# Two meta rows of an output projection, formed on VectorE and turned to channels through DRAM

## The chip, the cores and the metric

The kernel runs on one core of a Trainium2 chip. Its time is device time in microseconds. The kernel before was run three times: 1255.90, 1255.19 and 1255.82 us, a median of 1255.82. One more execution was taken with the hardware profiler, and all traces here are of such single executions.

A core has five engines that run their own instruction streams in order: TensorE (PE in the profile, with its weight loads as PEld), VectorE (DVE), ScalarE (ACT), GpSimd (POOL) and SyncE (SP), which issues most of the transfers. They wait for each other by semaphores.

## The reference

The program is one layer of a decoder trunk on 1,024 tokens of width 1,024, ahead of which stand 16 meta tokens. A first normalisation is followed by one wide projection; its columns feed an attention branch and a convolution branch, whose outputs are gated and added. What matters here comes after that:

```
mixed = sigmoid(g_attn) * y_attn + sigmoid(g_conv) * y_conv
h = layer_norm(ALPHA * h + mixed @ w_out, ln1_g, ln1_b)
up = causal_dwconv(h @ ffn_w_up, ffn_dw, ffn_dw_b)      # 3 taps: token t needs t-2, t-1, t
...
return h[:, N_META:]                                    # the meta tokens are dropped
```

The meta tokens' outputs are dropped, but the feed-forward convolution of the first real token reaches two tokens back. So after attention only the last two of the 16 meta tokens are still needed, and of those only `h` after `layer_norm`, as columns (one number per channel) at the left edge of the first token block. These are the two meta rows.

## The kernel before, in words

All matrix products are of float32 accuracy, made of reduced-precision passes: an operand is split into a rounded part `hi` and a remainder `lo` (`split`: a copy on ScalarE, then a subtraction on VectorE or GpSimd), and three products `hi*hi`, `hi*lo`, `lo*hi` are added in PSUM (`product`, L292 to L302).

The branches' projections run over eight stages `m` of 128 output channels (the loop that begins at L1080). In each, four column groups `g` of 256 or 258 tokens take two half-groups of 12 matmuls, one for each branch. Branch 0 writes to a pool of three PSUM banks, branch 1 to a pool of two. VectorE multiplies each with its gate (L1099, L1100), adds the two (L1101), and with ScalarE splits the sum into `mixed` (L1108, L1109). Group 0 holds the two meta tokens too; their 128 channels of `mixed` are kept in `pair[:, m]`, as `hi` and `lo`. During the same stages the eight 128x1024 tiles of `w_out` are loaded: four to parts of `FA` (`early`), two more that are split in stages 2 and 3 with the subtraction on GpSimd, and the last two into the weight buffers `wr`, split at the end.

Then come the row blocks (`out_rows`, L1230), in the order 3, -1, 7, 2, 6, 0, 4, 1, 5 (L1386). A row block is 128 tokens by 1,024 columns of `mixed @ w_out`, computed as two halves of 24 matmuls. VectorE adds the residual (L1253), takes statistics (L1254), and after a reciprocal root on ScalarE (L246) and three small steps it scales the rows (L1277). They are stored to `h1d` and, behind the first half of the next block, transposed on TensorE (`turn`, L1287) and copied by ScalarE into the feed-forward's operand in `FA` with gain and bias applied (L1300).

Block -1 is the two meta rows. Its stationary operand is `pair[:, k]`, four columns (two tokens, `hi` and `lo`) with `w_out`'s `hi`, and two columns with its `lo`: 16 matmuls of 512 columns in each half (L1264, L1265). ScalarE copies four rows out of PSUM (L1266); the lower two are moved beside the upper two by a small transfer, and VectorE adds both and the residual (L1270, L1272). After scaling, the two rows wait in a list and are turned together with block 2: eight transposes (L1287) and eight ScalarE steps of 128x2 into `edge`, which `edges` copies into the first two columns of `FA` (L1378).

After the row blocks follow the feed-forward's up products (L1499) and down products (L1637).

A scheduler orders each engine's instructions by their ranks and by its own estimate of when operands are ready; `after` adds an order between two instructions, `rank` sets a priority. The order is fixed when the kernel is built.

Of the kernel before, what the change touches and what calls it, by code (L numbers as in the profile page):

```python
# [99 lines left out]
def tile_hybrid_layer(  # L100
# [51 lines left out]
    sgd = dpool.tile([2, KC, P, U], F, name="sgd")  # L152
    h0d = dpool.tile([U, D], F, name="h0d")
    h1d = dpool.tile([S, D], F, name="h1d")
    fd = dpool.tile([FC, P, S], F, name="fd")

    td, sd = (dpool.tile([FH, P, 4 * 512], F, name=n) for n in ("td", "sd"))
# [860 lines left out]
    for g in range(3):  # L1018
# [8 lines left out]
    RW = wo_stack.enter_context(tc.tile_pool(name="rw", bufs=1, side="right", reuse_waits="tile")).tile(  # L1027
        [P, 2048], R, name="RW")
    RT = OB[:, 0:2048]


# [19 lines left out]
    def prep_wo(k, raw=None, behind=None):  # L1051
        if k < 4:
            hi, lo = OA[:, k * 2048:k * 2048 + 1024], OA[:, k * 2048 + 1024:k * 2048 + 2048]
        elif k < 6:
            hi, lo = ((RX, RW)[k - 4][:, x:x + 1024] for x in (0, 1024))
        else:
            hi, lo = (wsp_p.tile([P, D], R, name=n, tag=n) for n in ("whi", "wlo"))
        if raw is None:
            raw = wraw([P, D])
            load(raw, w_out_v[k])  # L1060
        split(raw, hi, lo, k < 4, behind)
        wo[k] = (hi, lo)

    pair = const.tile([P, KC, 4], R, name="pair")
    const.tile([P, 16], F, name="pad_e")
    g_next = [0]

    GS = [(FA, i * 516) for i in range(4)]
# [11 lines left out]
    for m in range(KC):  # L1080
        hi, lo = weights([P, KC, P], lambda raw: load(raw, w_ab[m]))

        def branch(i, g, tag, bufs):
            a, b = PG[g]
            ps = pat.tile([P, 512], F, name="ps_p", tag=tag, bufs=bufs)
            rhs = (oo, conv)[i]
            product(ps[:, :b - a], [(hi[:, 4 * i + k], lo[:, 4 * i + k], rhs(k, 0, a, b), rhs(k, 1, a, b))
                                    for k in range(4)])
            return ps[:, :b - a]

        def merge(g, psa, psb):
            a, b = PG[g]
            n = b - a
            with rank(RK_EVAC):
                t = gslot()[:, :, :n]
                ins = load(t, dram(sgd, m * P * U + a, [[U, P], [KC * P * U, 2], [1, n]]))

                ta, tb = t[:, 0], t[:, 1]
                nc.vector.scalar_tensor_tensor(ta, ta, 1.0, psa, OP.add, OP.mult)  # L1099
                nc.vector.scalar_tensor_tensor(tb, tb, 1.0, psb, OP.add, OP.mult)  # L1100
                nc.vector.tensor_tensor(ta, ta, tb, OP.add)  # L1101
                if g == 0:
                    nc.scalar.mul(pair[:, m, 0:2], ta[:, 0:2], 0.5)
                    nc.vector.scalar_tensor_tensor(pair[:, m, 2:4], ta[:, 0:2], 0.5, f32(pair[:, m, 0:2]),
                                                   OP.mult, OP.subtract)
# [3 lines left out]
                nc.vector.scalar_tensor_tensor(mixed2(g, m, 1), v, 0.5, f32(h), OP.mult, OP.subtract)  # L1109
            return ins, last_act  # L1110

        if m < KC - 1:
            for g in range(4):
                last_gate, last_act = merge(g, branch(0, g, "mm", 3), branch(1, g, "t", 2))
        else:
            pa = [branch(0, g, "mm", 3) if g < 3 else branch(0, g, "s", 2) for g in range(4)]
            for g in range(4):
                last_gate, last_act = merge(g, pa[g], branch(1, g, "t", 2))
        if m in (2, 3):
            raw = (FA[:, 4112:5136], OB[:, 3072:4096])[m - 2]  # L1120
            load(raw, w_out_v[m + 2])
            prep_wo(m + 2, raw, last_act)
        if m < 4:
            early.append(FA[:, W_AT[m]:W_AT[m] + 1024])
            after(load(early[m], w_out_v[m]), last_gate)
    for k in range(4):
        prep_wo(k, early[k])
    prep_wo(6)
    prep_wo(7)

# [99 lines left out]
    def out_rows(i, between=(), work=()):  # L1230


        n, u = (P, 2 + i * P) if i >= 0 else (2, 0)
        if n == P:
            o = r_next[0] % 2 * 1024
            r_next[0] += 1
            whole = RT[:, o:o + 1024]
            load(whole, h0d[u:u + n, :])
        else:
            whole = OB[:, 3072:4096]  # L1240
        r = whole[:n]
        order = WO_ORDER if i != 5 else (0, 1, 2, 3, 6, 7, 4, 5)
        turned = None
        st = small.tile([P, 2, 6], F, name="st")
        pin = line if i in (0, 4, 1, 5) else lambda ins: ins
        for half in range(2):
            hs = slice(half * 512, half * 512 + 512)
            ps = pat.tile([P, 512], F, name="ps_w", tag="mm", bufs=3)
            if n == P:
                last = product(ps, [(mixed(i, k, 0), mixed(i, k, 1), wo[k][0][:, hs], wo[k][1][:, hs])  # L1250
                                    for k in order], turned)
                with rank(RK_TURN):
                    pin(nc.vector.tensor_tensor(r[:, hs], ps, r[:, hs], OP.add))  # L1253
                    pin(nc.vector.bn_stats(st[:, half], r[:, hs]))  # L1254
                turned = None
                if len(between) > half:
                    turned = turn(*between[half], behind=[last])
                if half == 0:
                    for f, *x in work:
                        f(*x)  # L1260
                continue

            for j, k in enumerate(order):
                nc.tensor.matmul(ps[:4], pair[:, k], wo[k][0][:, hs], start=j == 0, stop=False)  # L1264
                last = nc.tensor.matmul(ps[:2], pair[:, k, 0:2], wo[k][1][:, hs], start=False, stop=j == KC - 1)  # L1265
            nc.scalar.copy(whole[:4, hs], ps[:4])  # L1266
        if n < P:
            q = FA[:4, 0:1024]
            load(q[0:2], h0d[0:2, :])
            nc.vector.tensor_tensor(r, r, q[0:2], OP.add)  # L1270
            load(q[0:2], whole[2:4])
            nc.vector.tensor_tensor(r, r, q[0:2], OP.add)  # L1272
        with rank(RK_TURN):
            (mu, rs), = ln_stats([(r, n)], half_stats=st if n == P else None)
            for a in (512, 0) if i == 5 else (None,):
                x = r if a is None else r[:, a:a + 512]
                ins = pin(nc.vector.tensor_scalar(x, x, mu, rs, OP.subtract, OP.mult))  # L1277
        if n == P:
            load(h1d[u - 2:u - 2 + P, :], r)
        return whole, n, ins  # L1280

    def turn(i, r, n, ins, banks=None, behind=None, upper=False):
        with rank(RK_TURN):
            for j, k0 in enumerate((4, 0) if upper else (0, 4)):
                ps = banks[j] if banks else pat.tile([P, 512], F, name="ps_h", tag="s", bufs=2)
                for k in range(4):
                    ins = nc.tensor.transpose(ps[:, k * P:(k + 1) * P], r[:, (k0 + k) * P:(k0 + k + 1) * P], ident)  # L1287
                    if behind:
                        after(ins, behind[-1])
                        behind.append(ins)  # L1290
                for k in range(k0, k0 + 4):
                    src = ps[:, (k - k0) * P:(k - k0) * P + n]
                    if n < P:
                        dst = edge[:, k]
                    else:
                        h, jj = divmod(i, 4)
                        sub = 0 if jj < 2 else 1
                        a = 2 + jj * P - SUB[sub][0]
                        dst = h1F(sub, h, k)[:, a:a + P]
                    nc.scalar.activation(dst, src, AF.Identity, bias=b1col(k), scale=g1col(k))  # L1300
        return behind[-1] if behind else None

# [71 lines left out]
    def edges():  # L1374
        with rank(RK_TURN):
            first, second = (FA[:, h * 2064:h * 2064 + 2064].rearrange("p (k n) -> p k n", n=258)[:, :, 0:2]
                             for h in range(2))
            nc.vector.tensor_copy(first, edge)  # L1378
            nc.vector.memset(second, 0.0)

    ahead = []
# [1 line left out]
            4: [(w_first, 2), (split_of, 1, BT2), (form_t4, 1)],  # L1383
            1: [(form_t3, 1), (w_first, 3)],
            5: [(form_t3, 0, EARLY), (form_t4, 0, EARLY)]}
    for i in (3, -1, 7, 2, 6, 0, 4, 1, 5):  # L1386
        if i == -1:
            two = (i, *out_rows(i))
# [402 lines left out]
```

## Time and profile before

| | |
|---|---|
| median of three runs | 1255.82 us |
| the profiled execution | 1255.65 us, its span 1253.9 us |
| mean granted TensorE clock | 0.999 |
| TensorE busy | 1241.6 us, 8,546 matmuls |
| VectorE busy | 1081.1 us, 1,876 instructions |
| ScalarE busy | 586.7 us, 1,056 instructions |
| GpSimd busy | 12.3 us, 11 instructions |
| projections / row blocks / up / down products | 416 to 510 / 503 to 610 / 607 to 1036 / from 1036 us |

How to read the lines: the page gives busy time, share of the span and count for each engine, and the span in 40 slices (tenths busy, 9 for 90% or more). A timeline row is start, duration, engine, line of the kernel, operation, output `<-` inputs, shape and count; brackets at its end give the idle time before it and what ended it. A matmul's duration runs from its start to the end of its way through the array; matmuls overlap, and the distance of two starts is what one costs. A group row gives count, busy us and the mean ns of one, then the idle time before. A wait row is engine and line `<-` what it waited for: total us, times, longest. A stretch row gives for each engine the busy us and count, then clock, share of the DMA engines and GB/s. A transfer row gives size and the median us from issue to landing.

### The profile page before, as it was taken

Reading aid. Unit: us, or ns where it says so; the run is one execution under the profiler, and the core shown is the slowest. Engines: PE = TensorE matmul, PEld = TensorE weight load, DVE = VectorE, ACT = ScalarE, POOL = GpSimd, SP = SyncE. Lnnn points to the kernel's source line nnn. Section 1 sums busy time; section 2 is a strip of 40 time slices with the busy share of each in tenths; the row PEclk is TensorE's granted clock in tenths of the full one; section 3 lists DMA queues with packets and bytes.
Section 4 is the critical chain, followed back from the end, with each engine's and each line's share of the span. In section 5 each row is a group of like instructions: output and inputs, shape, how many; then the busy total and the mean of one; then the engine's idle time right before and its main releaser. Section 6 shows DMA issues by size and latency. Waiting matters only on the chain.

```text
span 1253.9 us, 21702 instructions
## 1 busy us (share of the span) xinstructions
PE 1241.6 (99%) x8546; PEld 1174.7 (94%) x8546; DVE 1081.1 (86%) x1876; ACT 586.7 (47%) x1056; POOL 12.3 (1%) x11
## 2 busy tenths in 40 slices
PE   9999999999999999999999999999999999999997
PEld 8999999999999999788899999999999998888886
DVE  7899989999978786648899999999999986996697
ACT  7522345645465233235565555554455553545330
POOL 0000000000000010000000000000000000000000
PEclk9999999999999999999999999999999999999999
DMA  7293733332255565222145565553464569988722
GB/s 280 71 312 103 183 107 95 109 93 87 68 147 142 182 173 139 77 75 101 68 135 187 192 210 189 186 215 120 167 218 167 204 207 318 387 317 315 251 85 84
DMA packets 96152, 212.10 MB, mean 169 GB/s; under 512 B 10787, under 2 KB 35939, under 8 KB 95922
## 3 DMA queue, kind: packets, MB, share of 16 engines
q1 hardware_dynamic: 84282, 199.64, 48.1%
q10 hardware_dynamic: 11768, 11.08, 2.7%
q8 instruction: 67, 1.10, 0.4%
q14 instruction: 35, 0.29, 0.1%
HBM read 150.29 MB, written 62.70 MB: 170 GB/s over the span
## 4 chain that ended last, share of the span: by engine, by line
PE 95%; DVE 3%; DMA 1%; issue 1%; ACT 0%; SPq 0%; DVEq 0%
PE px L1499 15%; PE py L1499 10%; PE ps_x L1637 9%; PE ps_z L1637 7%; PE ps_z L300 7%; PE ps_z L301 7%; PE ps_z L296 7%; PE pw L1499 5%; PE pz L1499 5%; PE ps_p L301 2%; PE ps_p L296 2%; PE ps_p L300 2%; PE ps_w L301 2%; PE ps_w L296 2%; PE ps_w L300 2%; PE ps_z L512 2%
## 5 line engine op out<-in xcount | busy, mean ns | idle before, releaser
L665 DVE SCALAR_TENSOR_TENSOR FA<-cin,cols,FA 128x1026 f32<-128x1026 f32 x120 | 152.5, 1280 | 0.3
L296 PE MATMUL ps_z<-RHO,whi 128*128 128x384 f32 (+2 forms) x324 | 104.2, 322 | 0.0
L300 PE MATMUL ps_z<-RHC,whi 128*128 128x384 f32 (+2 forms) x324 | 104.1, 321 | 0.0
L300 PE MATMUL ps_z<-RHO,whi 128*128 128x384 f32 (+2 forms) x324 | 104.0, 321 | 0.0
L301 PE MATMUL ps_z<-RHC,wlo 128*128 128x384 f32 (+2 forms) x324 | 103.8, 320 | 0.0
L296 PE MATMUL ps_z<-RHC,whi 128*128 128x384 f32 (+2 forms) x324 | 103.7, 320 | 0.0
L301 PE MATMUL ps_z<-RHO,wlo 128*128 128x384 f32 (+2 forms) x324 | 103.7, 320 | 0.0
L267 ACT CAST whi<-wr 128x1024 fp32r<-128x1024 f32 x37 | 39.0, 1053 | 69.1 <-PE ps_z L300 52.2
L1317 ACT CAST RHO<-wr 128x512 fp32r<-128x512 f32 x94 | 56.9, 621 | 24.2 <-DVE wr L1335 13.6
L1318 DVE TENSOR_TENSOR RHO<-wr,RHO 128x512 fp32r<-128x512 f32 x94 | 63.8, 690 | 4.5 <-ACT RHO L1317 4.2
L296 PEld LDWEIGHTS ps_z<-RHO,whi 128*128 128x128 f32 x324 | 61.0, 188 | 0.6 <-issue 0.3
L296 PEld LDWEIGHTS ps_z<-RHC,whi 128*128 128x128 f32 x324 | 61.1, 188 | 0.2
L301 PEld LDWEIGHTS ps_z<-RHO,wlo 128*128 128x128 f32 x324 | 61.0, 188 | 0.2
L301 PEld LDWEIGHTS ps_z<-RHC,wlo 128*128 128x128 f32 x324 | 60.9, 188 | 0.2
L1335 DVE TENSOR_TENSOR wr<-wr 128x512 f32<-128x512 f32 x88 | 61.0, 693 | 0.2
L300 PEld LDWEIGHTS ps_z<-RHO,whi 128*128 128x128 f32 x324 | 61.0, 188 | 0.1
L300 PEld LDWEIGHTS ps_z<-RHC,whi 128*128 128x128 f32 x324 | 60.9, 188 | 0.1
L672 ACT ACTIVATE FA<-ps_z,cols 128x384 f32<-128x384 f32 (+1 forms) x48 | 26.1, 543 | 50.3 <-PE ps_z L301 49.3
L1511 ACT COPY FA<-px 128x514 f32<-128x514 f32 (+2 forms) x23 | 13.2, 572 | 73.3 <-PE px L1499 73.3
L270 DVE TENSOR_TENSOR wlo<-wr,whi 128x1024 fp32r<-128x1024 f32 x35 | 42.6, 1218 | 4.8 <-ACT whi L267 4.1
L1318 DVE TENSOR_TENSOR ws<-wr,ws 128x512 fp32r<-128x512 f32 x60 | 40.9, 690 | 5.5 <-ACT ws L1317 5.3
L1424 ACT ACTIVATE FA<-OB,cols 128x512 f32<-128x512 f32 x44 | 36.0, 817 | 13.6 <-DVE OB L1507 13.6
(466 smaller groups left out, 3520.7 us busy)
## 6 DMA issues: line engine op xcount, KB each, us to landing
wr<-in_w_up_dram SPq DMA_DIRECT2D x44, 512.0 KB, 3.8
wr<-in_w_z_dram SPq DMA_DIRECT2D x30, 512.0 KB, 4.3
fd<-FA SPq DMA_DIRECT2D x44, 256.0 KB, 2.0
OB<-in_w_down_dram SPq DMA_DIRECT2D x19, 512.0 KB, 4.8
qt<-qd SPq DMA_DIRECT2D x28, 256.0 KB, 4.1
sgd<-FA ACTq DMA_DIRECT2D x32, 192.0 KB, 3.1
td<-OB SPq DMA_DIRECT2D x12, 512.0 KB
sums<-fd SPq DMA_DIRECT2D x12, 512.0 KB
```

What stands on the lines that cost most here:

```text
L267: ins = nc.scalar.copy(hi, raw)
L270: return (nc.vector if quick else nc.gpsimd).tensor_tensor(lo, raw, f32(hi), OP.subtract)
L296: ins = nc.tensor.matmul(ps, ah, bh, start=i == 0, stop=False)
L300: nc.tensor.matmul(ps, ah, bl, start=False, stop=False)
L301: last = nc.tensor.matmul(ps, al, bh, start=False, stop=i == n - 1)
L665: nc.vector.scalar_tensor_tensor(acc[c], cin[:, j:j + U], wc, acc[c], OP.mult, OP.add)
L1317: nc.scalar.copy(hi, src)
L1318: ins = nc.vector.tensor_tensor(lo, src, f32(hi), OP.subtract)
L1335: ins = nc.vector.tensor_tensor(*x)
L1424: nc.scalar.activation(t, cc[:, 2:HW], AF.Identity, bias=ffw(3, o), scale=ffw(2, o))
L1499: ins = nc.tensor.matmul(o, x[:, ks], bmat(sub, q, hl, k), start=first and k + j == 0, stop=k == 3 and j == 2, skip_group_check=not first)
L1637: nc.tensor.matmul(banks[i], l[:, ts], r[:, ws], start=first and a and x + k == 0, stop=z and x == len(ops) - 1 and k == 2, skip_group_che ...
```

## The change

In words:

- `pair` is now float32 and holds the two tokens' channels as they are; the splitting step for it (L1104 before) goes.
- `two_rows(k)` forms the products on VectorE: for each of the two tokens, a tile `two` of 128x1024 takes up `w_out`'s raw tile `k` times the token's 128 channels, one factor per partition. Tile 0 is done on ScalarE, the others are multiply-adds on VectorE. Tiles 0 to 5 fall in the projection stages, tile 6 at their end, tile 7 behind block 3's scaling.
- The sum over partitions that is still missing is made by TensorE: both `two` tiles are split behind block 7's scaling, and eight matmuls with a selecting operand `sel` (ones in one column) bring token 0's sum to row 0 and token 1's to row 1.
- Block -1 moves behind block 2. Its rows come out of PSUM as two rows; one residual add is left of the two adds, and the small transfer goes.
- `turn` no longer treats two rows. The scaled rows are written to a DRAM buffer `ed` and read back in two transfers of 128x8 single elements into `edge`; `edges` applies gain and bias on VectorE.

```diff
-    pair = const.tile([P, KC, 4], R, name="pair")
+    pair = const.tile([P, KC, 4], F, name="pair")
+    sel = const.tile([P, 16], R, name="sel")
...
+    def two_rows(k, behind=None):
+        for t, a in enumerate(two_sum):
+            m = pair[:, k, t:t + 1]
+            if k == 0:
+                nc.scalar.activation(a, wo_raw[k], AF.Copy, scale=m)
+                continue
+            ins = nc.vector.scalar_tensor_tensor(a, wo_raw[k], m, a, OP.mult, OP.add)
+            if behind is not None:
+                after(ins, behind)
...
+        if m > 1:
+            with rank(RK_PROJ + 3000):
+                two_rows(m - 2)
...
-            for j, k in enumerate(order):
-                nc.tensor.matmul(ps[:4], pair[:, k], wo[k][0][:, hs], start=j == 0, stop=False)
-                last = nc.tensor.matmul(ps[:2], pair[:, k, 0:2], wo[k][1][:, hs], start=False, stop=j == KC - 1)
-            nc.scalar.copy(whole[:4, hs], ps[:4])
+            for j in range(4):
+                nc.tensor.matmul(ps[:2], sel[:, j // 2 * 2:j // 2 * 2 + 2], two_parts[j // 2][j % 2][:, hs],
+                                 start=j == 0, stop=j == 3)
+            nc.scalar.copy(r[:, hs], ps[:2])
...
+            load(ed, r)
+            for t in range(2):
+                load(edge[:, :, t], dram(ed, t * D, [[1, P], [P, KC]]))
...
-            nc.vector.tensor_copy(first, edge)
+            for t, c, op in ((edge, 58, OP.mult), (first, 66, OP.add)):
+                nc.vector.tensor_tensor(first, t, colA[:, c:c + KC].unsqueeze(2).to_broadcast([P, KC, 2]), op)
...
-    for i in (3, -1, 7, 2, 6, 0, 4, 1, 5):
+    for i in (3, 7, 2, -1, 6, 0, 4, 1, 5):
...
+        if i == 3:
+            two_rows(7, rows[2])
         if i == 7:
-            ahead.append(two)
+            for a, (hi, lo) in zip(two_sum, two_parts):
+                after(split(a, hi, lo, True), rows[2])
```

In the changed order of instructions, `edges` stands on VectorE between the two halves of block 6, and the eight `sel` matmuls stand between block 2's second half and block 6's first.

More of the change, by code (lines that the diff above doesn't have):

```diff
@@ L154, in tile_hybrid_layer @@
     h1d = dpool.tile([S, D], F, name="h1d")
+    ed = dpool.tile([2, D], F, name="ed")
     fd = dpool.tile([FC, P, S], F, name="fd")
@@ L1060, in prep_wo @@
             load(raw, w_out_v[k])
+        wo_raw[k] = raw
         split(raw, hi, lo, k < 4, behind)
         wo[k] = (hi, lo)
-    pair = const.tile([P, KC, 4], R, name="pair")
-    const.tile([P, 16], F, name="pad_e")
+    pair = const.tile([P, KC, 4], F, name="pair")
+    sel = const.tile([P, 16], R, name="sel")
+    nc.vector.memset(f32(sel), 0.0)
+    for t in range(2):
+        nc.vector.memset(f32(sel[:, 3 * t:3 * t + 1]), 1.0)
+    two_sum = [wo_p.tile([P, D], F, name=f"two{t}") for t in range(2)]
+    two_parts = [[OC[:, (2 * t + hl) * D:(2 * t + hl + 1) * D] for hl in range(2)] for t in range(2)]
+    wo_raw = {}
+    def two_rows(k, behind=None):
[7 more added lines that the diff above has]
+                after(ins, behind)
     g_next = [0]
@@ L1261, in out_rows @@
                 continue
-            for j, k in enumerate(order):
-                nc.tensor.matmul(ps[:4], pair[:, k], wo[k][0][:, hs], start=j == 0, stop=False)
-                last = nc.tensor.matmul(ps[:2], pair[:, k, 0:2], wo[k][1][:, hs], start=False, stop=j == KC - 1)
-            nc.scalar.copy(whole[:4, hs], ps[:4])
+            for j in range(4):
+                nc.tensor.matmul(ps[:2], sel[:, j // 2 * 2:j // 2 * 2 + 2], two_parts[j // 2][j % 2][:, hs],
+                                 start=j == 0, stop=j == 3)
+            nc.scalar.copy(r[:, hs], ps[:2])
         if n < P:
[L1268 to L1272, printed above, removed]
+            q = FA[:2, 0:1024]
+            load(q, h0d[0:2, :])
+            nc.vector.tensor_tensor(r, r, q, OP.add)
         with rank(RK_TURN):
@@ L1279, in out_rows @@
             load(h1d[u - 2:u - 2 + P, :], r)
+        else:
+            load(ed, r)
+            for t in range(2):
+                load(edge[:, :, t], dram(ed, t * D, [[1, P], [P, KC]]))
         return whole, n, ins
@@ L1291, in turn @@
                 for k in range(k0, k0 + 4):
[L1292 to L1299, printed above, removed]
+                    src = ps[:, (k - k0) * P:(k - k0 + 1) * P]
+                    h, jj = divmod(i, 4)
+                    sub = 0 if jj < 2 else 1
+                    a = 2 + jj * P - SUB[sub][0]
+                    dst = h1F(sub, h, k)[:, a:a + P]
                     nc.scalar.activation(dst, src, AF.Identity, bias=b1col(k), scale=g1col(k))
@@ L1385, in tile_hybrid_layer @@
             5: [(form_t3, 0, EARLY), (form_t4, 0, EARLY)]}
[L1386 removed]
+    for i in (3, 7, 2, -1, 6, 0, 4, 1, 5):
         if i == -1:
[L1388 removed]
+            out_rows(i)
             continue
```

8 lines of the change are left out of this document (4 added, 4 removed).

## The prediction

> **What bounds the kernel now.** I read the page's busy shares and slices first, then the chain that ended last, then TensorE's waits in the stage that the change touches.
>
> ```profile
> PE 1241.6 (99%) x8546; PEld 1174.7 (94%) x8546; DVE 1081.1 (86%) x1876; ACT 586.7 (47%) x1056; POOL 12.3 (1%) x11
> PE   9999999999999999999999999999999999999997
> PEclk9999999999999999999999999999999999999999
> PE 95%; DVE 3%; DMA 1%; issue 1%; ACT 0%; SPq 0%; DVEq 0%
> PE pw L1499 <- ACT FA L1300: 1.0, 1, 1.0
> ```
> TensorE is busy for 99% of the span and carries 95% of the last chain at full clock. The last line is the only wait of over 0.1 us that it has between 410 and 620 us, where the projections and the eight row blocks of `w_out` run. So a matmul taken out there is worth its whole slot, and a wait put in costs its whole length.
>
> **What TensorE loses and gains.** The timeline of TensorE around the meta rows:
>
> ```profile
> 515.48 0.40 PE L1264 MATMUL ps_w<-RX,pair 128*4 128x512 f32 x1
> ...
> 518.96 0.40 PE L301 MATMUL ps_w<-whi,RHC 128*128 128x512 f32 x1
> ...
> 524.06 0.40 PE L1265 MATMUL ps_w<-wlo,pair 128*2 128x512 f32 x1
> 524.29 0.39 PE L296 MATMUL ps_w<-RX,RHC 128*128 128x512 f32 x1
> ...
> 529.51 0.40 PE L301 MATMUL ps_w<-whi,RHC 128*128 128x512 f32 x1
> 529.74 1.04 PE L1287 MATMUL ps_h<-cols,OB 128*128 128x128 f32 x8
> ...
> 547.90 0.60 PE L1287 MATMUL ps_h<-cols,OB 128*128 128x128 f32 x4
> 548.25 0.48 PE L296 MATMUL ps_w<-RX,RHC 128*128 128x512 f32 x1
> ...
> 549.04 0.60 PE L1287 MATMUL ps_h<-cols,OB 128*128 128x128 f32 x4
> 549.40 0.48 PE L296 MATMUL ps_w<-RW,RHC 128*128 128x512 f32 x1
> ```
> Durations overlap here, so starts are what counts. From 515.48 to 524.29 lie 38 starts (32 of the meta rows, 6 of row block 3): 8.81/38 = 0.232 us each, so a stationary operand of two or four columns costs as much as one of 128. The change takes out 32 × 0.232 = 7.4 us, and the eight transposes at 547.90 and 549.04, 0.35 + 0.36 = 0.7 us. It puts in eight matmuls with `sel` as the stationary operand and 512 moving columns: 8 × 0.232 = 1.9 us. Net: 7.4 + 0.7 − 1.9 = **6.2 us less**.
>
> **What stood in the shadow of those 7.4 us.** Row block 3 is added, normalised and then transposed. In the rows above its last product starts at 518.96, the meta rows fill TensorE until 524.29, row block 7's first half until 529.74, and only then come block 3's transposes. VectorE and ScalarE meanwhile:
>
> ```profile
> 518.93 1.29 DVE L1253 TENSOR_TENSOR OB<-ps_w,OB 128x512 f32<-128x512 f32 x2 [4.73 <-PE ps_w L301]
> 520.14 1.28 DVE L1254 BATCH_NORM_STATS2 st<-OB 128x6 f32<-128x512 f32 x2
> 521.45 0.21 DVE L241 BATCH_NORM_AGGREGATE mv<-st 128x2 f32<-128x12 f32 x1
> 523.06 0.16 DVE L247 SCALAR_TENSOR_TENSOR sd<-mv,sd 128x1 f32<-128x1 f32 x1 [1.40 <-ACT sd L246]
> 523.64 0.81 DVE L1277 TENSOR_SCALAR OB<-OB,mv,sd 128x1024 f32<-128x1024 f32 x1
> ```
> ```profile
> 520.84 0.57 ACT L1266 COPY OB<-ps_w 4x512 f32<-4x512 f32 x1 [9.04 <-PE ps_w L1265]
> 521.43 1.28 ACT L246 ACT_TABLE_LOAD   x1
> 522.73 0.30 ACT L246 ACTIVATE sd<-mv,eps 128x1 f32<-128x1 f32 x1
> ```
> The block is ready at 524.45, 5 us ahead of its use. With the meta rows gone only block 7's first half lies in between, and 10 of its 24 products have already filled the place before block 3's last ones; 14 remain. With block 3's last product in the old place, TensorE reaches the transposes at 519.2 + 14 × 0.227 = 522.4 (0.227: 23 steps from 524.29 to 529.51). The chain gets shorter by about 1.05 us, since the table load no longer stands behind the copy of L1266 (523.06 becomes 522.0), and longer by two steps of 0.69 us (half of the x2 rows): the changed order puts the add and the statistics of block 7's first half ahead of block 3's scaling. 524.45 − 1.05 + 1.35 = 524.75. TensorE, which runs in order, waits 524.75 − 522.4 = **2.4 us**. Nothing fills it.
>
> **The products on VectorE.** Fourteen multiply-adds of 128x1024 are added, two per weight tile from the second on; the first tile's pair goes to ScalarE. Later come two splits (subtraction on VectorE, copy on ScalarE).
>
> ```profile
> L665 DVE SCALAR_TENSOR_TENSOR FA<-cin,cols,FA 128x1026 f32<-128x1026 f32 x120 | 152.5, 1280 | 0.3
> L270 DVE TENSOR_TENSOR wlo<-wr,whi 128x1024 fp32r<-128x1024 f32 x35 | 42.6, 1218 | 4.8 <-ACT whi L267 4.1
> L267 ACT CAST whi<-wr 128x1024 fp32r<-128x1024 f32 x37 | 39.0, 1053 | 69.1 <-PE ps_z L300 52.2
> 438.50:449.80 11.30, 11.30 (x98) 11.30 (x97) 7.63 (x18) 2.80 (x6) 0.00 (x0) 1.00 0.70 187
> 449.80:461.00 11.20, 11.20 (x99) 11.20 (x99) 9.63 (x18) 3.71 (x7) 2.44 (x1) 1.00 0.69 187
> 461.00:472.30 11.30, 11.30 (x97) 11.30 (x97) 9.59 (x18) 3.69 (x7) 2.39 (x1) 1.00 0.54 142
> ```
> The last three rows are stretches of about one projection stage: its ends, its length, then the busy time of TensorE, its weight loads, VectorE, ScalarE and GpSimd. At 1.28 us each, a pair adds 2.56 us to a stage of 11.25 us. In an ordinary stage VectorE goes from 7.63 to 10.2 and still fits; in the two stages with a GpSimd split it goes from 9.6 to 12.2, 0.95 too much each, 1.9 us of backlog together. TensorE feels that only where a PSUM bank is still unread when it comes round. The tighter pool has two banks, reused three half-groups (3 × 1.41 = 4.2 us, an eighth of a stage each) later; counted in the changed order, the reads run up to 4.6 us late in the second GpSimd stage, with 0.6 to 1 us of the next stage's products placed ahead as cover. Between 0 and 1.9 us; I take 0.3, by the cover. The splits (2 × 1.22) and the last pair fall behind blocks 7 and 3, where VectorE waited 4.73 us and more for TensorE: nothing. The dropped small steps on `pair` and the second add of L1272 gain nothing either; VectorE isn't the bound there. ScalarE's first pair (2 × 1.05, the cast L267's time) lies in 2.8 busy of 11.2: nothing.
>
> The GpSimd stage shows a block:
>
> ```profile
> 452.47 2.44 POOL L270 TENSOR_TENSOR RX<-FA,RX 128x1024 fp32r<-128x1024 f32 x1 [449.15 <-ACT RX L267]
> 452.55 2.65 DVE L1109 SCALAR_TENSOR_TENSOR RHC<-OB,RHC 128x256 fp32r<-128x256 f32 x1
> ```
> ```profile
> 441.13 0.42 DVE L1109 SCALAR_TENSOR_TENSOR RHC<-OB,RHC 128x256 fp32r<-128x256 f32 x1
> ...
> 503.12 0.39 PE L296 MATMUL ps_w<-RX,RHC 128*128 128x512 f32 x1
> ```
> The step takes 0.42 us in the stage before (441.13) and here lasts until GpSimd is through. The Trainium skill's page SBUF — State Buffer (Who interferes with whom) says that a VectorE step with two SBUF inputs and a GpSimd step that reads SBUF exclude each other, the first to start blocking the other; the two rows agree. By that rule the new multiply-adds can also hold up GpSimd, which would delay `RX` and `RW`, not needed before 503.12 us: the sum stays.
>
> **The way through DRAM.** `load(ed, r)` and two reads of 1,024 single elements each replace eight transposes and eight small ScalarE steps; `edges` then waits for the reads, on VectorE, ahead of row block 6's second half. The nearest rows:
>
> ```profile
> FA<-OB SPq DMA_DIRECT2D x1, 8.0 KB
> DVE OB L1272 <- DMA FA<-OB: 2.1, 1, 2.1
> bias<-vd SPq DMA_DIRECT2D x2, 512.0 KB, 11.7
> bias<-vd SPq DMA_DIRECT2D x2, 64.0 KB, 7.1
> 545.00:550.00 5.00, 5.00 (x28) 4.17 (x27) 1.60 (x3) 1.48 (x7) 0.00 (x0) 1.00 0.08 30
> 560.82 0.69 DVE L1253 TENSOR_TENSOR OB<-ps_w,OB 128x512 f32<-128x512 f32 x1 [4.92 <-PE ps_w L301]
> 563.43 0.81 DVE L1277 TENSOR_SCALAR OB<-OB,mv,sd 128x1024 f32<-128x1024 f32 x1
> ```
> Let P be the start of the eight new matmuls. ScalarE's copies end at P+2.6 (1.9, 0.2 of latency and 0.57). On VectorE follow the add (1.2 for its 1,024 columns), the two rows' statistics (1.3 and 0.2), block 2's three small steps and scaling (0.6 and 0.7), and the two rows' own (0.6 and 0.8): P+8.0. The write takes some 2.1 (the 8 KB row), issuing the two reads 1.0: P+11.1. Landing takes between 2.1 (8 KB) and 7.1 (the 64 KB load, also 1,024 pieces, of 64 bytes): P+13.2 to P+18.2. TensorE ends block 6's second half at P + 1.9 + 24 × 0.227 + 0.8 + 24 × 0.227 = P+13.6 and wants its transposes at P+19.05. An undisturbed block takes 3.4 us (560.82 to 564.24); with 0.4 for the steps of `edges`, landing after P+15.2 costs its excess: 0 to 3.0 us. Midway, 4.6, gives P+15.7: I take **0.5**. On SP, the store and the reads are queued ahead of block 6's store and block 4's residual only, not wanted for 10 us.
>
> **The sum.** −6.2 + 2.4 + 0.3 + 0.5 = −3.0 us. The profiled execution took 1255.65 (1253.9 of span and 1.75 around it), 0.17 under the median of 1255.82: 1252.65, which I give as 1252.7 for the median.
>
> **The rivals.** (1) Block 3's wait doesn't arise, because its halves are finished earlier or others fill the gap: −6.2, 1249.5. For it: today's 5 us of slack; against it: the slack is the removed work itself. (2) The backlog of VectorE reaches TensorE in the projections, its 1.9 and up to both GpSimd blocks (2.4 each): −3.3 + 1.9 to 4.8, 1254.2 to 1257. For it: 12.2 in 11.25; against it: five banks. (3) Slower: the single elements come late. VectorE stands before block 6's second half, and TensorE waits for its transposes. From a landing of 7.7 us after issue the gain is gone; at 11.7 (the 512 KB row, 1,024 pieces of 512 bytes) it is P+22.8, a wait of 7.6, and −3.5 + 7.6 = +4.1: 1259.8. For it: nothing in the trace reads 4-byte data elements; against it: only 4 KB move, in a stretch of light traffic (0.08 of the DMA engines from 545 to 550 us, second last figure of that row). (4) The gap of 2.4 us makes the clock fall for a few us: at half clock over 3.4 us, +1.7, 1254.4; the trace shows the clock full in all slices, with gaps of 1 us. The Trainium skill's TensorE: Matmul & The Clock Gate (Part 1) puts the idle window at about 3.4 us, by which 2.4 us is too short; no row here has such a gap.
>
> **How the numbers follow.** Forecast 0.45, (1) 0.15, (2) 0.18, (3) 0.14, (4) 0.08. A change of 0.2% (2.5 us), about what a measurement tells, puts the border at 1253.3. Faster: most of the forecast and (1), 0.55; same: the rest of it, (4), most of (2) and the start of (3), 0.28; slower 0.17. The likeliest case alone spans 1250.8 to 1254.5; the range reaches to (1) and into (2) and (3): 1249.4 to 1257.6.
>
> **What would show it.** Eight `sel` matmuls in place of 32; TensorE waiting about 2.4 us for L1298 ahead of block 3's transposes, the one new wait of that size; multiply-adds of 1.28 us; VectorE waiting 3 to 6 us for `edge`, and TensorE under 1 us at block 6's transposes. Waits of TensorE on `ps_p`, or a landing over 7 us, would make it wrong.

## The result and the profile after

The changed kernel took 1253.51 us (median of 14 runs, 1252.38 to 1256.07) against 1255.83 for the kernel before (14 runs beside it). The ratio is 0.9982, 95% interval 0.9975 to 0.9989: faster, by about 2.3 us. The profiled execution took 1252.68 us, 0.03 from the sum of the prediction's terms; its span is 1250.9 where it was 1253.9.

The median hides something that one execution can't show. The 14 times fall into two groups that go with the mean clock granted to TensorE: seven at 0.998 or 0.999 with a median of 1252.72, and seven at 0.996 or 0.997 with a median of 1254.24. The 44 runs of the kernel before for which the clock was listed stand at 0.998 or 0.999, all of them.

The profile's page of the changed kernel, the busy shares:

```profile
PE 1236.1 (99%) x8514; PEld 1172.3 (94%) x8514; DVE 1093.0 (87%) x1887; ACT 587.5 (47%) x1052; POOL 12.7 (1%) x11
```

TensorE still bounds the kernel and has 5.5 us less to do, with 32 matmuls fewer. The waits of TensorE between 410 and 620 us of the changed kernel (line waited for, then total, times and longest, in us):

```profile
PE ps_h L1312 <- DVE OB L1298: 2.2, 1, 2.2
PE pw L1525 <- ACT FA L1322: 1.0, 1, 1.0
PE px L1525 <- ACT OB L1537: 0.3, 1, 0.3
```

The wait of 1.0 us was there before. The large new one is block 3's, 2.2 us; the third, 0.3 us, is new too and small; none is on `ps_p`. The timelines of TensorE and VectorE around it, and from block -1 to block 6:

```profile
522.38 0.39 PE L302 MATMUL ps_w<-whi,RHC 128*128 128x512 f32 x1
524.99 1.09 PE L1312 MATMUL ps_h<-cols,OB 128*128 128x128 f32 x8 [2.23 <-DVE OB L1298]
543.19 2.02 PE L1287 MATMUL ps_w<-OC,sel 128*2 128x512 f32 x8
562.10 0.39 PE L302 MATMUL ps_w<-whi,RHO 128*128 128x512 f32 x1
562.46 1.07 PE L1312 MATMUL ps_h<-cols,OB 128*128 128x128 f32 x8
```
```profile
524.14 0.80 DVE L1298 TENSOR_SCALAR OB<-OB,mv,sd 128x1024 f32<-128x1024 f32 x1
...
549.99 0.80 DVE L1298 TENSOR_SCALAR OB<-OB,mv,sd 2x1024 f32<-2x1024 f32 x1
...
558.60 0.18 DVE L1401 TENSOR_TENSOR FA<-edge,cols 128x16 f32<-128x16 f32 x1 [6.45 <-DMA edge<-ed]
...
561.50 0.81 DVE L1298 TENSOR_SCALAR OB<-OB,mv,sd 128x1024 f32<-128x1024 f32 x1
```

The transposes of block 3 start as soon as VectorE has scaled its rows. Further on VectorE stands still for 6.45 us until `edge` has come from DRAM, and then scales block 6 by 562.31. Its transposes start 0.36 us after the last product (562.46 − 562.10), where ahead of the other blocks that step takes 0.23, so TensorE loses 0.13 us there, too little for the list of waits. The projection stages, in the same columns as before:

```profile
438.50:449.80 11.30, 11.30 (x98) 11.30 (x97) 9.46 (x19) 2.80 (x6) 0.00 (x0) 1.00 0.69 184
449.80:461.00 11.20, 11.20 (x97) 11.20 (x97) 10.28 (x17) 3.48 (x7) 2.57 (x1) 1.00 0.64 174
461.00:472.30 11.30, 11.30 (x100) 11.30 (x99) 10.87 (x20) 3.57 (x8) 2.59 (x1) 1.00 0.54 138
```

VectorE is up to 96% busy there (10.87 of 11.30), and TensorE has no wait there.

One measure serves for all kernels below: the stretch of TensorE from the first projection matmul into `ps_p` to the first up product into `px`. It holds all that the change touches and leaves out the start-up and the feed-forward. No edit changes TensorE's work in these two, and yet in the ten profiled executions the stretch starts between 415.17 and 416.47 us, and what follows it takes 646.1 to 647.8 us. Its two ends, before and then after:

```profile
416.04 0.28 PE L296 MATMUL ps_p<-OA,whi 128*128 128x258 f32 x1
607.76 1.58 PE L1499 MATMUL px<-OC,RHO 128*128 128x256 f32 x12
```
```profile
415.90 0.28 PE L297 MATMUL ps_p<-OA,whi 128*128 128x258 f32 x1
604.19 1.58 PE L1525 MATMUL px<-OC,RHO 128*128 128x256 f32 x12
```

That is 191.72 and 188.29 us: 3.4 us gained in the stretch. In each experiment "the stretch" is this figure, read off in the same way.

### The profile page after: what moved, and what is told of

It reads as the page before. It is cut to its first block, busy times and chain, and to the rows that moved or that the text cites. A ratio compares the mean times of both kernels' runs of the same rounds, so it can differ in the third digit from the quotient of the medians.

```text
span 1250.9 us, 21668 instructions
## 1 busy us (share of the span) xinstructions
PE 1236.1 (99%) x8514; PEld 1172.3 (94%) x8514; DVE 1093.0 (87%) x1887; ACT 587.5 (47%) x1052; POOL 12.7 (1%) x11
## 4 chain that ended last, share of the span: by engine, by line
PE 94%; DVE 3%; DMA 2%; issue 1%; ACT 0%; SPq 0%; DVEq 0%
PE px L1525 15%; PE py L1525 9%; PE ps_x L1663 9%; PE ps_z L1663 7%; PE ps_z L301 7%; PE ps_z L302 7%; PE ps_z L297 7%; PE pz L1525 5%; PE pw L1525 5%; PE ps_p L297 2%; PE ps_p L302 2%; PE ps_p L301 2%; PE ps_w L302 2%; PE ps_w L297 2%; PE ps_w L301 2%; PE ps_z L513 2%
## 5 line engine op out<-in xcount | busy, mean ns | idle before, releaser
L1339 ACT CAST ws<-wr 128x512 fp32r<-128x512 f32 x60 | 36.3, 620 | 13.0 <-DVE wr L1357 7.4
```

The source lines that it names most:

```text
L1339: nc.scalar.copy(hi, src)
```

## The experiments

The theory after the result: the two large terms of the sum were about right, and the gap that the removed work left at block 3 costs more than its own length, because in some runs TensorE's clock falls behind it.

**1. The gap closed.** Block 3's transposes go behind block 7's second half instead of its first.

```
-                if len(between) > half:
+                if len(between) > half and between[half]:
...
-        rows = out_rows(i, ahead, work.get(i, ()))
+        rows = out_rows(i, ahead if i != 7 else [None] + ahead, work.get(i, ()))
```

> The changed kernel with block 3's eight transposes put behind the second half of block 7 instead of behind its first half; nothing is left out. Theory (the 2.23 us wait of TensorE at block 3's transposes is the only thing that the removed meta rows laid bare, and the wait is also what lowers the clock in about half of the runs of the changed kernel, 1252.7 at 0.999 against 1254.2 at 0.997): the wait goes, TensorE is busy through 522 to 525 us, the time is 1252.7 - 2.2 = 1250.5, and all runs lie within 0.5 us of it at a clock of 0.998 or more. Rival A (the two groups of times come from something else, the reads of single elements for one): 1250.5 and 1252.0, again in about equal numbers. Rival B (the wait only moves to a later place, since the blocks' VectorE work is late everywhere): no gain, 1252.7.

Measured: 1250.66 us (5 runs, 1249.39 to 1250.94), ratio to the kernel before 0.9958 (0.9944 to 0.9971). The clock was 0.998 in all five. The stretch is 186.15 us, 2.1 less than the changed kernel's. Beside the old wait of 1.0 us TensorE has one small wait, now at block 6's transposes. It stands here ahead of the row for the time in which the gap lay, beneath which stands the changed kernel's row for that time:

```profile
PE ps_h L1312 <- DVE OB L1298: 0.2, 1, 0.2
```
```profile
522.50:525.20 2.70, 2.70 (x14) 2.23 (x13) 2.52 (x6) 0.00 (x0) 0.00 (x0) 1.00 0.00 0
```
```profile
522.50:525.20 2.70, 0.47 (x4) 0.21 (x3) 2.52 (x6) 0.00 (x0) 0.00 (x0) 1.00 0.00 0
```

VectorE does the same 2.52 us of work in both, but TensorE has other products meanwhile. The gap was worth its length, so rival B falls. With it the runs of low clock are gone, in these five runs and in the five of the eighth experiment, which has no gap either; so rival A falls too. The times do not lie as close together as was expected (1.5 us from end to end, the kernel before has 1.3); what spreads them at one clock was not looked into.

**2. The move alone, in the kernel before.** Only the place of block -1 changes; its 32 matmuls and the transposes stay.

```
-    for i in (3, -1, 7, 2, 6, 0, 4, 1, 5):
+    for i in (3, 7, 2, -1, 6, 0, 4, 1, 5):
```

> The kernel before, with the meta rows' 32 matmuls put behind row block 2, as in the changed kernel, and formed and transposed as before; nothing is left out. Theory (the meta rows' 7.4 us covered block 3's normalisation, and moving them is enough to open the gap): TensorE waits 2 to 3 us at block 3's transposes, the time rises by that, 1255.8 + 2.2 to 3 = 1258.0 to 1258.8, and by some 1.5 more in runs in which the clock falls. Rival (the gap comes from the changed kernel's added VectorE work, 14 multiply-adds of 1.28 us): no wait over 0.5 us there, 1255.8.

Measured: 1258.28 us (8 runs, 1257.66 to 1260.12), ratio 1.0026 (1.0016 to 1.0036). Five runs at 0.998 or more have a median of 1257.86, three at 0.997 or less 1259.48. The stretch is 194.09, 2.4 more than before. TensorE's wait:

```profile
PE ps_h L1287 <- DVE OB L1277: 2.2, 1, 2.2
```

The same 2.2 us without one of the new multiply-adds. So the wait comes from the meta rows' matmuls no longer standing between block 3's last product and its transposes, not from the added VectorE work, and it brings the lower clock along.

**3. The gap doubled.** Three multiplications by one lengthen VectorE's work on block 3's rows.

```
                 ins = pin(nc.vector.tensor_scalar(x, x, mu, rs, OP.subtract, OP.mult))
+                for _ in range(3 if i == 3 else 0):
+                    ins = nc.vector.tensor_scalar(x, x, 1.0, None, OP.mult)
```

> The changed kernel with three more multiplications by one (0.8 us each, 128x1024) on VectorE between block 3's scaling and its transposes, so that the wait of 2.23 us becomes about 4.6; nothing is left out. Theory (a gap lowers the clock for some us, at 2.2 us only in about half of the runs, which is 1.5 us): the clock falls in nearly every run, 1252.7 + 2.4 + 1.5 = 1256.6, all runs in one group at 0.997 or less, and the trace shows a granted clock below 1 behind the gap. Rival (the gap has nothing to do with the two groups): 1255.1 and 1256.6 in equal numbers.

Measured: 1256.52 us (11 runs, 1255.10 to 1258.73), the clock at 0.997 or less in all eleven. The wait is 4.41 us (first row below), the stretch 192.48, 4.2 longer than the changed kernel's: 2.2 of wait and 2.0 more, for which one window at half clock (half of 3.41, 1.7) and a second wait of 0.3 are at hand. Its two new waits, and three stretches of 3.41 us behind one another, where the third last figure of a row is the granted clock:

```profile
PE ps_h L1314 <- DVE OB L1300: 4.4, 1, 4.4
PE ps_h L1314 <- DVE OB L1298: 0.3, 1, 0.3
```
```profile
523.89:527.30 3.41, 0.22 (x2) 0.22 (x3) 3.31 (x6) 0.00 (x0) 0.00 (x0) 1.00 0.00 0
527.31:530.71 3.40, 3.40 (x13) 3.01 (x12) 2.10 (x2) 2.58 (x6) 0.00 (x0) 0.50 0.51 175
530.72:534.10 3.38, 3.38 (x16) 2.75 (x16) 0.00 (x0) 2.19 (x5) 0.00 (x0) 1.00 0.75 247
```

Behind a stretch with 0.22 us of matmul the clock is at half for 3.41 us and then full again. That the gap and the lower clock belong together is shown. Only "one group" was wrong: the runs spread over 3.6 us, and three stood at 0.995. One such stretch lowers the mean by 0.5 × 3.41/1255 = 0.0014, so two in one run would do that. No trace here shows such a run of this kernel; the seventh experiment's trace shows two such stretches, at a mean of 0.995.

**4. The transposes back.** The two rows are turned on TensorE again, with block 2's; the meta rows are still formed on VectorE.

```
-            load(ed, r)
-            for t in range(2):
-                load(edge[:, :, t], dram(ed, t * D, [[1, P], [P, KC]]))
...
-            for t, c, op in ((edge, 58, OP.mult), (first, 66, OP.add)):
-                nc.vector.tensor_tensor(first, t, colA[:, c:c + KC].unsqueeze(2).to_broadcast([P, KC, 2]), op)
+            nc.vector.tensor_copy(first, edge)
...
-            out_rows(i)
+            ahead.append((i, *out_rows(i)))
```

> The changed kernel with the way through DRAM undone: the two rows are turned by eight transposes and ScalarE steps as before, together with row block 2's, and the meta rows are still formed on VectorE; nothing is left out. Theory (the way through DRAM costs TensorE nothing now and saves the transposes): +0.7 us, 1253.4 against 1252.7 at equal clock, VectorE's wait of 6.45 us for edge gone, and the two groups of times stay, since the gap at block 3 stays. Rival (the reads of single elements hold up something that the trace doesn't show as a wait of TensorE, or cause the second group): 1252.7 or less, or one group only.

Measured: 1254.50 us (11 runs, 1252.79 to 1255.08) beside 1255.33 for the kernel before. Eight runs at 0.997 have a median of 1254.55, three above it 1253.46 (they lie far apart, at 1252.79, 1253.46 and 1255.08). Both groups are about 1 us nearer to the kernel before than the changed kernel's: 1.9 and 0.8 us below it, where those were 3.1 and 1.6. The stretch is 189.07, 0.8 longer. VectorE's wait for `edge` is down to 1.0 us, now for ScalarE's steps:

```profile
DVE FA L1399 <- ACT edge L1321: 1.0, 1, 1.0
```

So by the stretch the way through DRAM gains what the eight transposes took (step: 0.7); the times alone could not tell, since the interval of the ratio, 0.9982 to 1.0000, overlaps with the changed kernel's. And the two groups are there without it, so it does not cause them.

**5. The changed kernel again**, without an edit, on the chip of the next three.

> The changed kernel once more, beside the others on one chip. Theory (the granted clock is decided in windows of 3.41 us, since the trace of the longer gap had it at half for 3.413 us and every stretch of full clock was a whole number of 3.413 us; in the changed kernel's trace the gap of 2.2 us lay across the border of two windows, 1.1 us in each, and the clock held): runs of two kinds again, 1.5 us apart, those with the border inside the gap fast at 0.998 or more; if the profiled one is of the slower kind, its trace shows 3.41 us at half clock that begins at the end of the window which held nearly the whole gap. Rival (the slower runs have no such stretch): the mean clock is lower without a fall behind the gap.

Measured: 1253.19 us (10 runs, 1251.43 to 1255.14) against 1255.50, ratio 0.9980 (0.9971 to 0.9989). Five runs at 0.998 or 0.999 have a median of 1252.52, five at 0.997 or 0.996 have 1253.86. The profiled one was of the quicker kind again (1252.66), so this run shows no fall; the next one does, behind the very same gap. The stretch is 188.12, against 188.29 in the first profile. Most of the difference is block 6: here its rows were scaled and its transposes started at

```profile
560.06 0.81 DVE L1298 TENSOR_SCALAR OB<-OB,mv,sd 128x1024 f32<-128x1024 f32 x1
562.16 1.03 PE L1312 MATMUL ps_h<-cols,OB 128*128 128x128 f32 x8
```

so VectorE was through 1.29 us early and TensorE lost nothing. How late `edge` comes differs from execution to execution of the same kernel.

**6. One more hop through DRAM.** The two rows are copied once more before they are read as single elements.

```
-            load(ed, r)
+            load(ed0, r)
+            load(ed, ed0)
```

> The changed kernel with one more copy from DRAM to DRAM (8 KB) between the write of the two rows and the reads of single elements, so that edge lands some 2 us later; nothing is left out. Theory (the scaling of block 6's second half now ends 0.15 us ahead of its transposes, so hardly any slack is left): VectorE's wait for edge goes from 6.45 to about 8.5 us, TensorE waits about 2 us at block 6's transposes, the time rises by 2 us and by 1.5 more in runs in which that second gap lowers the clock as well: 1254.6 to 1256.1 against the changed kernel's 1252.7. Rival (VectorE has hidden slack, for instance the read lands early enough): within 0.5 us of the changed kernel.

Measured: 1254.15 us (10 runs, 1252.26 to 1256.34): 1253.62 at the higher clock (4 runs), 1255.59 at the lower (6 runs), so 1.1 and 1.7 us more than the changed kernel beside it. The profiled execution is one of the lower kind. Its transposes of block 6 and VectorE ahead of them:

```profile
565.80 1.06 PE L1314 MATMUL ps_h<-cols,OB 128*128 128x128 f32 x8 [1.14 <-DVE OB L1299]
```
```profile
559.25 0.69 DVE L1277 TENSOR_TENSOR OB<-ps_w,OB 128x512 f32<-128x512 f32 x1 [4.94 <-PE ps_w L303]
562.87 0.18 DVE L1403 TENSOR_TENSOR FA<-edge,cols 128x16 f32<-128x16 f32 x1 [2.92 <-DMA edge<-ed]
```

The `sel` matmuls start at 545.36 here. Counted from them, the steps on `edge` start 2.1 us later than in the changed kernel (17.5 us against 15.4). TensorE feels 1.2 of it: its step to the transposes is 1.53 us (565.80 − 564.27) in place of 0.36. The rest went because the edit changed the order as well: the add of block 6's second half now stands ahead of the steps that wait, and from them to the scaled rows it takes 2.78 us in place of 3.71. So there was no slack in these two executions, and the expected 2 us were too much by that reordering. The fifth experiment's execution had 1.29 us of slack, so the theory holds for some executions and the rival for others.

This profile also holds what the last one didn't. Around block 3's wait of 2.23 us (523.33 to 525.56), the next stretch and the long one behind it:

```profile
523.00:526.41 3.41, 1.18 (x10) 0.85 (x9) 3.20 (x6) 0.10 (x1) 0.00 (x0) 1.00 0.02 10
526.42:529.83 3.41, 3.41 (x11) 2.73 (x9) 1.47 (x2) 3.41 (x9) 0.00 (x0) 0.50 0.63 216
529.84:1250.04 720.20, 713.81 (x4989) 662.67 (x4988) 624.32 (x995) 349.74 (x556) 0.00 (x0) 1.00 0.54 192
```

In the traces read here the clock changes only at multiples of 3.413 us: the full stretch of 720.2 is 211 of them, the one ahead of the fall (4.18 to 526.41) 153, and the changed kernel's (5.04 to 1247.49) 364. So the borders at which it is decided can be counted back from the fall at the end of any trace. In the changed kernel's own profile, with the same 2.23 us, that fall comes at 1247.49, and 212 windows earlier lies 523.87, in the middle of the gap:

```profile
520.46:523.87 3.41, 2.30 (x11) 1.57 (x9) 2.79 (x9) 0.30 (x1) 0.00 (x0) 1.00 0.00 0
523.87:527.28 3.41, 2.29 (x14) 2.07 (x15) 3.41 (x4) 1.53 (x5) 0.00 (x0) 1.00 0.38 149
527.28:1247.49 720.21, 714.07 (x4991) 662.97 (x4989) 625.45 (x997) 351.77 (x560) 0.00 (x0) 1.00 0.54 192
1247.50:1250.90 3.40, 0.00 (x0) 0.00 (x0) 0.23 (x1) 0.00 (x0) 0.00 (x0) 0.50 0.41 154
```

TensorE was busy for 2.3 us in each of the two windows, and the clock held. In the fifth experiment's trace, counted in the same way, one window had 1.64 us, and the clock held. The fourth experiment comes nearest to the limit, and it held too:

```profile
520.82:524.23 3.41, 1.57 (x7) 0.95 (x6) 2.79 (x8) 0.29 (x1) 0.00 (x0) 1.00 0.00 0
```

With 1.18 us of matmul in a window of 3.41 the next window ran at half clock, with 1.57 it did not. If the border falls anywhere with the same chance, a gap of 2.23 us lies wholly in one window in (3.41 − 2.23)/3.41 = 35% of the cases; with the border at 1.57, that is 1.84 us of idle, it is (3.41 − 2.23 + 2 × 0.39)/3.41 = 57%. Over the five kernels with this gap 29 of 53 runs were at 0.997 or less, 55%. Only one of the 29 was profiled, the one above; that the others had the same fall is inferred from their mean clock and their times.

**7. The products twice.** Each multiply-add is followed by a second one with a column of zeros, except the last tile's pair behind block 3 (the added line stands in the branch without `behind`): 12 more, not 14.

```
+    nc.vector.memset(pair, 0.0)
...
             ins = nc.vector.scalar_tensor_tensor(a, wo_raw[k], m, a, OP.mult, OP.add)
             if behind is not None:
                 after(ins, behind)
+            else:
+                nc.vector.scalar_tensor_tensor(a, wo_raw[k], pair[:, k, 2:3], a, OP.mult, OP.add)
```

> The changed kernel with every one of the 14 multiply-adds done twice, the second time by a column of zeros, so that the two rows come out the same and VectorE has 1.28 us more for each; nothing is left out. Theory (five banks and the placing of the products ahead hide a backlog of up to about a microsecond, and the changed kernel used up nearly none of it): VectorE's load of a projection stage goes from 10.3 to 12.8 us in 11.25, TensorE waits at ps_p in the later stages for about 1.5 us each, and the time rises by 5 to 11 us. Rival (TensorE isn't reached because VectorE catches up in the stage behind): under 1 us.

Measured: 1262.32 us (4 runs, 1261.31 to 1262.90), ratio 1.0054 (1.0039 to 1.0070), 9.1 over the changed kernel beside it. TensorE's waits, and two stages:

```profile
PE ps_h L1315 <- DVE OB L1301: 5.0, 1, 5.0
PE ps_p L297 <- DVE OB L1123: 3.5, 3, 1.5
```
```profile
461.00:472.30 11.30, 8.83 (x73) 8.42 (x72) 10.25 (x18) 2.92 (x5) 0.11 (x1) 1.00 0.47 152
...
483.50:494.80 11.30, 10.62 (x91) 10.62 (x92) 11.30 (x22) 2.61 (x6) 0.00 (x0) 1.00 0.44 118
```

Twice the products is too much: VectorE is full from 472.3 us on (second row), TensorE waits for its banks, and what is left of the backlog falls on block 3, whose wait goes from 2.2 to 5.0 us. In the first row VectorE was not full: it stood 1.37 us for a load of gates just before TensorE's first wait, so not all of the 3.5 us is its own work. Behind a window with 0.07 us of matmul the clock is at half for two windows:

```profile
529.63:533.04 3.41, 1.75 (x9) 1.75 (x9) 3.10 (x6) 0.71 (x3) 0.00 (x0) 0.50 0.29 114
533.04:536.45 3.41, 3.41 (x10) 2.66 (x9) 0.58 (x1) 3.41 (x9) 0.00 (x0) 0.50 0.57 197
```

The first of them, with 1.75 us of matmul at half clock, was not enough to bring the clock back. 3.5 + 2.8 + 2.6 (half of the 5.2 us of matmul at half clock) = 8.9 of the 9.5 us by which the stretch grows to 197.83. The time is in the expected range, but only 3.5 us of it come by the expected way. The changed kernel's load fits and 2.6 us more in each stage do not; where in between VectorE's limit lies was not tried.

**8. The gap closed, and the wait for `edge` put later.** As in the first experiment, and VectorE's two steps on `edge` are ordered behind block 0's scaling.

```
+                after(nc.vector.tensor_tensor(first, t, colA[:, c:c + KC].unsqueeze(2).to_broadcast([P, KC, 2]), op),
+                      edge_behind[0])
...
+        if i == 0:
+            edge_behind = [rows[2]]
```

> The changed kernel with block 3's transposes behind block 7's second half, as in the run that removed the gap, and VectorE's steps that wait for edge ordered behind block 0's scaling, so that VectorE no longer stands before block 6's second half; nothing is left out. Theory (the way through DRAM costs TensorE nothing any more): VectorE's wait of 6.45 us for edge goes and the time is the same as without this step, 1250.7 within 0.3 us. Rival (the wait for edge still delays something of block 6 that TensorE meets): 0.3 to 1 us less.

Measured: 1249.74 us (5 runs, 1249.36 to 1251.44), ratio 0.9956 (0.9943 to 0.9968), the clock at 0.998 or more in all five. The one wait of TensorE left in the stretch is the old one, 1.0 us at `pw`.

The stretch is 185.69, 0.46 less than in the first experiment. There the step from the last product to block 6's transposes takes 0.62 us (559.65 to 560.27), here 0.23 (559.88 to 560.11), which is 0.4 of it. So the wait for `edge` did cost a little there, by the rival's account, though the times of the two (1249.36 to 1251.44 and 1249.39 to 1250.94) overlap. Both beat the changed kernel by 2 us and more, and the kernel before by 0.4%.

## Why the prediction came out as it did

**The bound and the 6.2 us.** Right. The eighth experiment, without any new wait of TensorE, has a stretch 191.72 − 185.69 = 6.0 us shorter than before.

**The wait at block 3, 2.4 us.** Right in cause, place and size: 2.23 us. The last product ahead of it starts at 522.38 and ends at 522.77, and the rows are ready at 524.94 where the step had 524.75. The step counted TensorE by starts; so counted, the transposes could have followed 0.23 us behind the last product, at 522.61 where it had 522.4, and the wait costs 524.99 − 522.61 = 2.4 us. The second experiment shows that the lost cover makes it.

**The products on VectorE, 0.3 us.** They cost nothing. The two stages with a GpSimd split came to 10.28 and 10.87 us of VectorE work where the step had 12.2, so no backlog arose, and rival (2) did not happen. In place of 6 × 1.28 = 7.7 us, the three stretches together rose by 3.8 (from 26.85 to 30.61). VectorE's groups by line from 438.5 to 472.3 us, before and after:

```profile
L1109 DVE SCALAR_TENSOR_TENSOR RHC<-OB,RHC 128x256 fp32r<-128x256 f32 x6 | 6.9, 1145 | 0.3 <-ACT RHC L1108 0.3
L1101 DVE TENSOR_TENSOR OB<-OB 128x256 f32<-128x256 f32 (+1 forms) x12 | 5.1, 427 | 0.4
...
L1109 DVE SCALAR_TENSOR_TENSOR RHO<-OB,RHO 128x256 fp32r<-128x256 f32 x6 | 2.5, 421 | 0.3
L1104 DVE SCALAR_TENSOR_TENSOR pair<-OB,pair 128x2 fp32r<-128x2 f32 x3 | 0.5, 159 | 0.0
```
```profile
L1121 DVE TENSOR_TENSOR OB<-OB 128x256 f32<-128x256 f32 (+1 forms) x12 | 8.5, 718 | 0.3
L1082 DVE SCALAR_TENSOR_TENSOR two<-FA,pair,two 128x1024 f32<-128x1024 f32 x6 | 7.4, 1283 | 0.8 <-DMA FA<-in_w_out_dram 0.8
...
L1127 DVE SCALAR_TENSOR_TENSOR RHO<-OB,RHO 128x256 fp32r<-128x256 f32 x5 | 2.1, 419 | 0.0
L1127 DVE SCALAR_TENSOR_TENSOR RHC<-OB,RHC 128x256 fp32r<-128x256 f32 x5 | 2.1, 417 | 0.0
```

The splits of `pair` are gone (0.5). Two of the twelve steps of L1109 (now L1127) fall outside (0.8). And the time for which VectorE stands beside a GpSimd split, 4.4 us before (9.4 less 12 × 0.42, at L1109), is 3.4 after (8.5 less 5.1, at L1121). The rest, 1.6, I can't assign to a line; overlapping durations, which count twice in a sum over lines but not in the busy time, are a part of it.

**The way through DRAM, 0.5 us.** The two rows were scaled at P+7.6 (step: 8.0), with P the start of the `sel` matmuls at 543.19, and `edge` was used at P+15.4 (step: 15.7, the threshold being 15.2). It cost 0.13 us in the profiled execution and nothing in the fifth experiment's, which was 1.29 us early. That the sum of the steps came so close is luck, since two of its terms are off and cancel. The transfers were issued like this:

```profile
550.86 0.24 SPq L111 DMA_DIRECT2D ed<-OB  x1
554.01 0.32 SPq L111 DMA_DIRECT2D OB<-h0d  x1
554.38 1.05 SPq L111 DMA_DIRECT2D edge<-ed  x2
```

From the write's issue to the reads' it took 3.5 us, where the step had 2.1. Block 0's residual (512 KB, the second row) stands ahead of the reads in SyncE's queue, and the step left it out: its buffer is block 2's, by the profile SyncE waited 2.8 us there for block 2's store, and the reads followed 0.37 us after that load's issue. Whether the write alone would have held them as long is not shown. In the fifth experiment's execution it took 2.4 us (550.69 to 553.07), in the eighth's 4.1 (548.64 to 552.78). From the end of the reads' issue to their use, on the other hand, it took 3.2 us (555.43 to 558.60) where the step had 4.6. The reads took 3.9 us from issue to landing, between the ends of 2.1 and 7.1; rival (3) needed 7.7 and did not happen. The traffic was not light, as the step had it: the DMA engines' share was 0.80 to 1.02 from 555 to 558 us. In the sixth experiment a landing 2.1 us later cost TensorE 1.2 us, in an order that is easier by 0.9.

**The clock.** This is the step that failed. Rival (4) was put at 0.08 and applies to about half of the runs. Its price, 1.7 us for one window at half clock, was right: the stretch of the sixth experiment is 191.10 − 188.29 = 2.8 us longer than the changed kernel's, 1.2 of it wait and 1.6 the clock; between the groups of the changed kernel's runs it is 1.5 and 1.3 us, in the other three kernels with this gap 1.1 to 2.0. What failed is the condition. The gap was weighed against a full idle window, as the Trainium skill's TensorE: Matmul & The Clock Gate has it (Part 1, and no idle gaps above about 3 us in Why this matters for your kernels). The page's free-running window of 3,413 ns agrees with the runs; that a window must be idle throughout does not, for 2.23 us of idle in it were enough, and so it hangs on where the border falls.

**The sum.** That the profiled execution met it to 0.03 us is luck: two differences cancel. The stretch gained 3.4 us where the sum had 3.0, since of the two small charges, 0.3 and 0.5, only 0.13 was due. What lies behind the stretch took 0.6 longer (1253.9 − 607.76 = 646.1 before, 1250.9 − 604.19 = 646.7 after), of which 0.3 is the third wait quoted above; the changed kernel run again had it too (0.7). This part went from 646.1 to 647.8 over the ten profiled executions, so whether the change causes the 0.6 is not shown. The median lies 0.8 above the forecast because half of the runs carry the 1.5 us of the clock. By the prediction's own border of 1253.3 us, a median of 1253.51 counts as "same" (0.28) and not as the likelier "faster" (0.55); 14 runs on each side can tell a smaller change than its 0.2%: the interval of the ratio leaves out 1.

## What to carry to other kernels

Work that is taken off the bounding engine may be the cover of another chain: look for what it stands in front of, and count what the next consumer will find ready; here 2.2 of 6.2 us were lost that way, and a step put half a block later gave them back. Price a new gap of TensorE not by its length alone but by its share of a 3.41 us window, and read the clock of several runs, since one profile can show only one of the two outcomes. When a change fills an engine to 96% of a stage, the next such change may be the one that costs: here the same work once more did.

## What the runs showed of the hardware

- The granted clock fell to half for one window of 3.41 us behind a window with 0.22 or 1.18 us of matmul (third and sixth experiment), and held behind windows with 1.57, 1.64 and 2.3 (fourth, fifth, the changed kernel). Behind a window with 0.07 us it stayed at half for two, the first of which had only 1.75 us of matmul (seventh). A single wait of 2.23 us is enough, by the mean clock in about half of the runs.
- Two reads of 1,024 single 4-byte elements each from DRAM landed 3.9 us after issue, right behind a load of 512 KB; one copy of 8 KB from DRAM to DRAM put 3.1 us between its own issue (556.62) and that of the reads behind it (559.75).
